# Causal masks moved from TensorE to a VectorE pass, and a token-stationary compression, in a two-layer hybrid transformer

## The chip, the cores and the metric

The kernel runs on one core of one Trainium2 chip. The metric is the device time of one execution in microseconds (us). The core has TensorE (PE in the profile, its weight loads PEld), VectorE (DVE), ScalarE (ACT), GpSimd (POOL) and SyncE (SP, which issues most transfers). Each engine works through its own queue in order and waits on semaphores of the others.

## The reference, cut to what matters

The model has two layers over 512 tokens of width 1024, in float32: an even layer (MoBA and differential attention, 16 score maps), an odd layer (NSA attention, 16 query heads with a selected and a window branch, 32 score maps), and a mixture of experts (MoE) after each. The change touches the causal softmax, which every score map goes through, and the compression of keys and values in the odd layer:

```python
s_own = jnp.where(kpos[None, :] <= qpos[:, None], s_own, NEG_INF)
p = jax.nn.softmax(jnp.concatenate([s_sel, s_own], axis=-1), axis=-1)

def compress_blocks(t, pos_emb, w1, b1, w2, b2):
    idx = jnp.arange(nc)[:, None] * CMP_STRIDE + jnp.arange(CMP_BLOCK)[None, :]   # stride 16, blocks of 32
    blocks = t[:, :, idx, :] + pos_emb.astype(t.dtype)
    hid = jax.nn.gelu(jnp.einsum('bgnld,ldf->bgnf', blocks, w1.reshape(CMP_BLOCK, d, -1)) + b1)
    return jnp.einsum('bgnf,fe->bgne', hid, w2) + b2
```

With 512 tokens all past blocks are selected, so each score map is a causal 512 x 512 one. The adaptive norms take `silu(c) @ ada_w`; the change also touches how `silu(c)` is laid out for it.

## The kernel before

The work runs in stages: modulation and the first projections (0 to 87 us), even attention with its output projection (87 to 345), MoE (to 541), the odd layer's compressions and projections (to about 655), odd attention with its output projection (to 985), MoE (to the end). Weights stream in through a pool of five tiles `w` of 512 KB.

A projection (`product`, line 332) is three matmuls per weight piece, with 256 or 304 columns: weights and activations are split into a high and a low part (`wh`, `wl`, `hTh`, `hTl`) by a cast on ACT (L299) and a subtraction on DVE or POOL (L301).

Scores are computed by `Attn.scores`, per head and per tile i of 128 queries, over n = 128, 256, 384 or 512 keys. Two matmuls (L493) write a PSUM bank `psS` (three banks), a third of 128 columns in bfloat16 (L495) adds the triangular mask `c_k_cmask` to the last 128 columns through the identity `identb`. DVE reduces the bank to the negated maximum `nm` (L497); ACT reads the bank again and writes `exp(s + nm)` into the tile `P` with its row sum in `sm` (L499). Tiles P come from four pools P0 to P3 by width, each with four buffers. DVE inverts the sums (L637, L943, L944), POOL scales P (L507), PE transposes P into `psT` (L520), ACT or DVE copies that to `PT` (L168, L171), and PE multiplies `PT` with the values (L528, L672). These last steps of a head pair stand behind the scores of the next pair. There are 16 + 32 maps with four tiles each: 64 tiles in the even and 128 in the odd layer, 192 in all. While attention runs, the next projection and the modulation units for later (`ada_unit`, L221 and L223, eight DVE passes each) are interleaved as background steps.

The compression (`compress`, L789) runs twice, for keys and values. Per pair of 32 steps of `l` it takes 128 tokens blocks (4 groups x 32, read from `cT` with a stride of 16) against 256 hidden units; the weights are the stationary side, in two halves `fo`, and 64 matmuls in all feed 128 columns each. A float32 matmul shows as two records in the trace. The result `hid` has hidden units on the partitions; bias, gelu and a second matmul follow.

The order on every engine is made at build time by a list scheduler, which goes by priorities and a model of durations. So an edit moves instructions elsewhere too.

Of the kernel before, what the change touches and what calls it, by code (L numbers as in the profile page):

```python
# [9 lines left out]
F32 = mybir.dt.float32  # L10
F32R = mybir.dt.float32r
BF = mybir.dt.bfloat16
I32 = mybir.dt.int32
AF = mybir.ActivationFunctionType
ALU = mybir.AluOpType
AX = mybir.AxisListType

D = 1024
S = 512
NT = 4  # L20
KC = 8
# [3 lines left out]
CAP = 96  # L25
SLOT_TILES = NEXP * CAP // 128
BIG = 8192.0
N_ADA = (3, 7, 7, 7)
N_ADA1 = (2, 2, 4, 3, 5)
PER0 = 6  # L30
# [43 lines left out]
def hybrid_kernel(ctx: ExitStack, tc: tile.TileContext, A: dict, out: bass.AP, dbg=None):  # L74
    nc = tc.nc
# [5 lines left out]
    cst = ctx.enter_context(mkpool("cst"))  # L81
# [4 lines left out]
    def ps(tag, dt=F32):  # L86
        return pp.tile([128, 512], dt, name="ps" + tag, tag=tag, bufs={"S": 3, "P": 2, "T": 2, "O": 1}[tag])
# [26 lines left out]
    ident = identr.bitcast(F32)  # L114
# [10 lines left out]

    late = []

    def load_const(name, shape, dt=F32):

        o = cst.tile(shape, dt, name="c_" + name)  # L130

        def load(pool):
            t = o
            if dt != F32:
                t = pool.tile(shape, F32, name="ctmp", tag=f"P{(shape[1] - 1) // 128}", bufs=4)
            tc.keep_in_program_order(nc.scalar.dma_start(t, A[name]))
            if dt != F32:
                nc.vector.tensor_copy(o, t)
        late.append(load)
        return o  # L140

    ropec = load_const("k_ropec", [128, NT, 16])
    ropes = load_const("k_ropes", [128, NT, 16])
    cmask = load_const("k_cmask", [128, 128], BF)
    zmask = load_const("k_zmask", [128, NT])
    tri = load_const("k_tri", [128, 128], BF)
    iotas = load_const("k_iota", [128, CAP], BF)
# [26 lines left out]
    ct = cst.tile([128, KC], F32, name="ct")  # L174
# [2 lines left out]
    nc.scalar.activation(ce, ct, AF.Exp, scale=-1.0)  # L177
    nc.vector.tensor_scalar(ce, ce, 1.0, None, op0=ALU.add)
    nc.vector.reciprocal(ce, ce)
    cs = cst.tile([128, KC, 32], F32, name="cs")  # L180
    nc.gpsimd.memset(cs, 0.0)
    nc.vector.tensor_tensor(cs[:, :, 0:1], ct[:, :, None], ce[:, :, None], op=ALU.mult)

    modp = [[dr.tile([1, D], F32, name=f"modp{l}_{p}") for p in range(6)] for l in range(2)]
    modg = [[dr.tile([1, D], F32, name=f"modg{l}_{p}") for p in range(2)] for l in range(2)]
# [18 lines left out]
    def ada_half(l, part, c, keep):  # L204

        p = ps("S")
        ts = []
        for q in range(2):
            ts.append(raw_piece(A["ada_w"][l], q, part * D + c * 256, 256))
        for q in QO:  # L210
            for k in range(4):
                nc.tensor.matmul(p[32 * k:32 * k + 32, :256], cs[:, 4 * q + k, :], ts[q][:, k, :],
                                 start=(q == QO[0]), stop=(q == QO[1]), tile_position=(0, 32 * k))
        evac(keep, p[:, :256], 256)

    def ada_unit(l, part, c, pool):


        a = g1[:, c * 256:(c + 1) * 256]
        ts = [raw_piece(A["ada_w"][l], q, part * D + c * 256, 256) for q in range(2)]  # L220
        nc.vector.tensor_scalar(a, ts[0][:, 0, :], cs[:, 0, 0:1], None, op0=ALU.mult)  # L221
        for k in range(1, KC):
            nc.vector.scalar_tensor_tensor(a, ts[k // 4][:, k % 4, :], cs[:, k, 0:1], a, op0=ALU.mult, op1=ALU.add)  # L223
        cost(0, 2600)
        if c == 3:
            p = ps("S")
            for j in range(4):
                nc.tensor.matmul(p[32 * j:32 * j + 32, :256], ones1.to_broadcast([128, 32]),
                                 g1[:, j * 256:(j + 1) * 256], start=True, stop=True, tile_position=(0, 32 * j))
            r = pool.tile([128, 256], F32, name="adap", tag="raw", bufs=2)  # L230
            evac(r, p[:, :256], 256)
            nc.sync.dma_start(modp[l][part].rearrange("a (j c) -> (a j) c", j=4), r[0:128:32, :])
            if part in (2, 5):
                nc.sync.dma_start(modg[l][part // 5].rearrange("a (p k) -> p (a k)", k=KC), mod_col(l, part, f"g{l}_{part}"))
# [175 lines left out]
    class Attn:  # L410
# [69 lines left out]

        def scores(self, qh, kh):

            pool = self.pool
            sm = pool.tile([128, NT], F32, name="sm", tag="sm", bufs=6)
            P = []
            for i in range(NT):
                n = (i + 1) * 128
                tc.cur_priority -= SCP
                if i != 1:
                    bank = ps("S")  # L490
                s = bank[:, 128:384] if i == 1 else bank
                for v in range(2):
                    nc.tensor.matmul(s[:, :n], qh[:, i * 128:(i + 1) * 128], kh[:, v, :n],  # L493
                                     start=(v == 0), stop=False)
                nc.tensor.matmul(s[:, i * 128:n], identb, cmask, start=False, stop=True)  # L495
                nm = pool.tile([128, 1], F32, name="nm", tag="nm", bufs=4)
                nc.vector.tensor_reduce(nm, s[:, :n], axis=AX.X, op=ALU.max, negate=True)  # L497
                e = pool.tile([128, n], F32, name="P", tag=f"P{i}", bufs=4)
                nc.scalar.activation(e, s[:, :n], AF.Exp, bias=nm, accum_out=sm[:, i:i + 1])  # L499
                cost(n / 1.2 + 240, n / 0.96 + 65)  # L500
                P.append(e)
                tc.cur_priority += SCP
            return P, sm
# [31 lines left out]
    def even_attn(l, bp, ns, ada, mlp):  # L535
        with mkpool(f"at{l}") as pool, mkpool(f"top{l}") as top:
# [26 lines left out]
            def affine(c):  # L563

                k2 = slice(2 * c, 2 * c + 2)
                p = ps("O")
                for j in range(2):
                    for k in range(2):
                        nc.tensor.matmul(p[:, 2 * j + k:2 * j + k + 1], parts[1 - j][:, k * 128:(k + 1) * 128], ones1,
                                         start=True, stop=True)  # L570
                nc.vector.tensor_tensor(sb[:, :, k2], p[:, 0:4].rearrange("p (j k) -> p j k", j=2), cols[:, 0:2, k2],
                                        op=ALU.add)
                nc.vector.scalar_tensor_tensor(sb[:, 0, k2], sb[:, 0, k2], 1.0, cols[:, 2, k2], op0=ALU.add, op1=ALU.mult)
# [155 lines left out]
    def odd_attn(l, bp, ns, ada, mlp):  # L729
        s1, b1 = mod_affine(l, 0, 1, A["norm1_g"][l], f"a{l}")  # L730
        with mkpool(f"at{l}") as pool, mkpool(f"top{l}") as top:
# [45 lines left out]

            def compress(a):
                cT = cT2[:, a]
                hid = ps("S")  # L780
                w1 = A["od_cmp_w1"][0, a].rearrange("(h l d) f -> h d l f", h=2, l=16)
                for q in range(4):
                    wt = wp.tile([128, 4, 256], F32, name="w", tag="w", bufs=WB)
                    for hf in range(2):
                        nc.sync.dma_start(wt[64 * hf:64 * hf + 64], w1[hf, :, 4 * q:4 * q + 4, :])
                    for fo in range(2):
                        for li in range(4):
                            lp = 4 * q + li
                            nc.tensor.matmul(hid[:, fo * 128:(fo + 1) * 128], wt[:, li, fo::2],  # L789
                                             cT[:, :, lp::16],  # L790
                                             start=(lp == 0 and fo == 0), stop=(lp == 15),
                                             skip_group_check=True)
                b1c = small([128, 2], "b1c")
                nc.sync.dma_start(b1c, A["od_cmp_b1"][0, a].rearrange("(p o) -> p o", o=2))
                nc.vector.tensor_tensor(b1c, b1c, hid[:, 31:256:128], op=ALU.add)
# [873 lines left out]
```

## Time and profile before

| | |
|---|---|
| median of 3 runs | 1183.71 us (1183.18 to 1186.62) |
| profiled execution | 1184.13 us, span 1182.4 us |
| PE busy | 1089.0 us, 92% of the span |
| DVE busy | 609.0 us, 52% |
| ACT busy | 503.9 us, 43% |
| POOL busy | 279.7 us, 24% |
| mean granted TensorE clock | 0.957 |

The span runs from the first to the last instruction of the profiled execution. Busy time is the union of an engine's instructions. The ends of matmuls are modelled, so their starts say more than their lengths. The queries used below cut the span into windows, name what an engine waited for, and list instructions in order of time.

### The profile page before, as it was taken

What the parts mean: (1) busy time and instruction counts of PE and PEld (TensorE: products, weight loads), DVE (VectorE), ACT (ScalarE), POOL (GpSimd) and SP (SyncE); (2) the same over time, 40 slices, a digit from 0 to 9 for tenths busy, and PEclk for the clock granted to TensorE, in tenths of its full rate; (3) what the DMA queues carried; (4) which work ended last, traced back from release to release, by engine and by line L of the source; (5) the groups of instructions that cost most, each with busy time, mean ns of one, the idle gap of its engine ahead of it and who ended that gap; (6) DMA issues with size and microseconds to landing.
All of it is one profiled execution on the core that took longest, in us unless ns stands there. A gap on an engine that the chain in (4) does not pass through costs nothing. (4 is left out here: it accounts for less than half of the span.)

```text
span 1182.4 us, 21909 instructions
## 1 busy us (share of the span) xinstructions
PE 1089.0 (92%) x8375; PEld 746.2 (63%) x8376; DVE 609.0 (52%) x1602; ACT 503.9 (43%) x1268; POOL 279.7 (24%) x362
## 2 busy tenths in 40 slices
PE   5899999989989899996999998998999998989994
PEld 3798889878764333335999977664577573433332
DVE  2587979884335233226227587536675325322234
ACT  2245656665432222214334565665745442213222
POOL 2200010333231211122001222333434223211223
PEclk8999899999999899996999999998999998989997
DMA  9864657631395899774366354201411094989857
GB/s 272 261 211 154 193 168 217 196 126 55 135 413 163 321 333 410 271 173 95 96 161 195 109 183 122 81 10 37 126 47 62 1 389 185 313 324 385 331 142 180
DMA packets 146086, 226.00 MB, mean 191 GB/s; under 512 B 31822, under 2 KB 116750, under 8 KB 141872
## 3 DMA queue, kind: packets, MB, share of 16 engines
q1 hardware_dynamic: 134400, 195.46, 49.3%
q0 software_dynamic: 10080, 28.46, 8.3%
q8 instruction: 69, 1.13, 0.4%
q10 hardware_dynamic: 1488, 0.55, 0.2%
q14 instruction: 49, 0.40, 0.1%
HBM read 212.73 MB, written 18.93 MB: 196 GB/s over the span
## 5 line engine op out<-in xcount | busy, mean ns | idle before, releaser
L332 PE MATMUL psP<-wh,hTh 128*128 128x256 f32 (+1 forms) x656 | 191.1, 297 | 6.6 <-ACT wh L299 2.8
L332 PE MATMUL psP<-wh,hTl 128*128 128x256 f32 (+1 forms) x656 | 187.2, 289 | 0.4 <-DVE hTl L301 0.4
L332 PE MATMUL psP<-wl,hTh 128*128 128x256 f32 (+1 forms) x656 | 183.0, 290 | 1.3 <-DVE wl L301 1.1
L1256 PE MATMUL psS<-gu,xT 128*32 128x512 f32 x1536 | 176.7, 605 | 0.3
L223 DVE SCALAR_TENSOR_TENSOR g<-w,cs,g 128x256 f32<-128x256 f32 x280 | 140.5, 526 | 2.8 <-DMA w<-in_ada_w_dram 1.7
L507 POOL TENSOR_SCALAR P<-P,sm 128x128 f32<-128x128 f32 (+3 forms) x160 | 97.4, 627 | 153.2 <-DVE sm L944 61.1
L332 PEld LDWEIGHTS psP<-wh,hTh 128*128 128x128 f32 x656 | 127.0, 195 | 8.8 <-ACT wh L299 3.2
L301 POOL TENSOR_TENSOR wl<-w,wh 128x512 fp32r<-128x512 f32 (+1 forms) x38 | 51.2, 1346 | 327.4 <-ACT wh L299 275.1
L332 PEld LDWEIGHTS psP<-wh,hTl 128*128 128x128 f32 x656 | 126.9, 193 | 2.0 <-issue 1.2
L497 DVE TENSOR_REDUCE nm<-psS 128x1 f32<-128x128 f32 x192 | 85.8, 484 | 80.2 <-PE psS L495 75.4
L332 PEld LDWEIGHTS psP<-wl,hTh 128*128 128x128 f32 x656 | 124.3, 194 | 4.3 <-DVE wl L301 3.0
L499 ACT ACTIVATE P<-psS,nm 128x128 f32<-128x128 f32 x192 | 101.6, 534 | 55.0 <-DVE nm L497 53.9
L299 ACT CAST wh<-w 128x512 fp32r<-128x512 f32 (+1 forms) x124 | 75.0, 609 | 111.5 <-PE psP L332 55.5
L1256 PEld LDWEIGHTS psS<-gu,xT 128*32 128x32 f32 x1536 | 55.3, 111 | 100.3 <-issue 92.1
L493 PE MATMUL psS<-kT,qT 128*128 128x512 f32 (+3 forms) x384 | 101.5, 355 | 2.5 <-ACT P L499 2.3
L332 PE MATMUL psP<-wh,o 128*128 128x256 f32 x480 | 95.6, 293 | 0.9 <-ACT o L299 0.7
L301 DVE TENSOR_TENSOR wl<-w,wh 128x512 fp32r<-128x512 f32 (+1 forms) x86 | 58.2, 677 | 63.4 <-ACT wh L299 61.1
L1278 PE MATMUL psP<-dn,sT 128*32 128x512 f32 x768 | 87.8, 595 | 1.0 <-ACT sT L1271 0.8
L168 ACT COPY PT<-psT 128x384 f32<-128x384 f32 (+1 forms) x125 | 62.8, 518 | 47.4 <-PE psT L520 46.7
L332 PEld LDWEIGHTS psP<-wh,o 128*128 128x128 f32 x480 | 75.7, 193 | 9.1 <-issue 5.7
L520 PE MATMUL psT<-identr,P 128*128 128x128 f32 x440 | 72.3, 286 | 3.4 <-ACT PT L168 2.9
L1227 ACT ACTIVATE xT<-psT,bm,sm 128x128 f32<-128x128 f32 x96 | 36.2, 457 | 88.8 <-PE psT L1246 88.8
(334 smaller groups left out, 1801.2 us busy)
## 6 DMA issues: line engine op xcount, KB each, us to landing
w<-in_ada_w_dram SPq DMA_DIRECT2D x96, 512.0 KB
gu<-in_moe_w_gate_dram SPq DMA_DIRECT2D x64, 512.0 KB
gu<-in_moe_w_up_dram SPq DMA_DIRECT2D x64, 512.0 KB
dn<-in_moe_w_down_dram SPq DMA_DIRECT2D x32, 1024.0 KB
w<-in_ev_w_in_dram SPq DMA_DIRECT2D x20, 512.0 KB
w<-in_od_w_in_dram SPq DMA_DIRECT2D x18, 512.0 KB
X<-yD POOLq DMA_DIRECT2D x16, 512.0 KB, 8.3
w<-in_ev_w_out_dram SPq DMA_DIRECT2D x8, 512.0 KB
```

What stands on the lines that cost most here:

```text
L168: nc.scalar.copy(o, i)
L223: nc.vector.scalar_tensor_tensor(a, ts[k // 4][:, k % 4, :], cs[:, k, 0:1], a, op0=ALU.mult, op1=ALU.add)
L299: nc.scalar.copy(hi, src)
L301: o = e.tensor_tensor(lo, src, hi.bitcast(F32), op=ALU.subtract)
L332: nc.tensor.matmul(dst, xx[:, k, tk], ww, start=(k == 0 and v == 0 and i % per == 0), stop=(k == 4 * len(qs) - 1 and v == 2), skip_group_c ...
L493: nc.tensor.matmul(s[:, :n], qh[:, i * 128:(i + 1) * 128], kh[:, v, :n], start=(v == 0), stop=False)
L497: nc.vector.tensor_reduce(nm, s[:, :n], axis=AX.X, op=ALU.max, negate=True)
L499: nc.scalar.activation(e, s[:, :n], AF.Exp, bias=nm, accum_out=sm[:, i:i + 1])
L507: nc.gpsimd.tensor_scalar(P[i], P[i], sm[:, i:i + 1], 1.0, op0=ALU.mult, op1=ALU.mult)
L520: nc.tensor.transpose(t[:, o:o + 128], P[i][:, j * 128:(j + 1) * 128], ident)
L1256: nc.tensor.matmul(hp[c], xT[:, k, c], gu(k), start=(k == 0), stop=(k == KC - 1), tile_position=(0, 32 * q))
L1278: nc.tensor.matmul(yp[g], sT[:, f, g], dn(f, c), start=(f == 0), stop=(f == 1), tile_position=(0, 32 * q))
```

## The change

1. The mask matmul goes. DVE runs one pass per tile instead of the reduce: it reads the scores from PSUM and the mask from SBUF, writes `-(s + mask)` into P and keeps the minimum, which is the negated maximum. This pass shows as two instructions, the pass and the read-out of its one value per partition. The exponential then works in place on P, with scale -1. `cmask` becomes 512 columns wide, 384 zeros and the triangle, so that its last n columns fit any tile.
2. In the compression the tokens become the stationary side and the weights are fed, 256 contiguous columns at a time: 32 matmuls. The result has tokens on the partitions; it is copied to SBUF (`hb`) and transposed back by four transpositions into `psT`.
3. `cs` (the activated `c`) loses its zero padding to 32 columns and is broadcast instead, so all 32 rows of a modulation product are equal, and the sum over them uses 1/32 (`part1`) instead of ones.

```diff
+    cmask = cst.tile([128, 512], BF, name="cmask")
+    nc.gpsimd.memset(cmask[:, 0:384], 0.0)
+    load_const("k_cmask", [128, 128], BF, cmask[:, 384:512])
...
-    cs = cst.tile([128, KC, 32], F32, name="cs")
-    nc.gpsimd.memset(cs, 0.0)
-    nc.vector.tensor_tensor(cs[:, :, 0:1], ct[:, :, None], ce[:, :, None], op=ALU.mult)
+    cs = cst.tile([128, KC], F32, name="cs")
+    nc.vector.tensor_tensor(cs, ct, ce, op=ALU.mult)
+    part1 = cst.tile([128, 1], F32, name="part1")
+    nc.gpsimd.memset(part1, 1.0 / 32)
...
                 for v in range(2):
                     nc.tensor.matmul(s[:, :n], qh[:, i * 128:(i + 1) * 128], kh[:, v, :n],
-                                     start=(v == 0), stop=False)
-                nc.tensor.matmul(s[:, i * 128:n], identb, cmask, start=False, stop=True)
+                                     start=(v == 0), stop=(v == 1))
                 nm = pool.tile([128, 1], F32, name="nm", tag="nm", bufs=4)
-                nc.vector.tensor_reduce(nm, s[:, :n], axis=AX.X, op=ALU.max, negate=True)
                 e = pool.tile([128, n], F32, name="P", tag=f"P{i}", bufs=4)
-                nc.scalar.activation(e, s[:, :n], AF.Exp, bias=nm, accum_out=sm[:, i:i + 1])
+                nc.vector.tensor_tensor_reduce(e, s[:, :n], cmask[:, 512 - n:], -1.0, -MASKED, ALU.add, ALU.min, nm)
+                nc.scalar.activation(e, e, AF.Exp, bias=nm, scale=-1.0, accum_out=sm[:, i:i + 1])
...
-                    for fo in range(2):
-                        for li in range(4):
-                            lp = 4 * q + li
-                            nc.tensor.matmul(hid[:, fo * 128:(fo + 1) * 128], wt[:, li, fo::2],
-                                             cT[:, :, lp::16],
-                                             start=(lp == 0 and fo == 0), stop=(lp == 15),
-                                             skip_group_check=True)
+                    for li in range(4):
+                        lp = 4 * q + li
+                        nc.tensor.matmul(hw[:, :256], cT[:, :, lp::16], wt[:, li, :], start=(lp == 0), stop=(lp == 15))
+
+                hb = top.tile([128, 256], F32, name="hb", tag="raw", bufs=2)
+                evac(hb, hw[:, :256], 256)
+                hid = ps("T")
+                for fo in range(2):
+                    nc.tensor.transpose(hid[:, fo * 128:(fo + 1) * 128], hb[:, fo::2], ident)
```

Nine lines more in the file move later line numbers: L332 becomes L339, L493 L501, L497 L505, L499 L506, L507 L514, L520 L527, L528 L535, L789 L795, the transpositions of `hb` are L801.

The first place is PE at the first compression of the odd layer; L771 (L778) are transpositions of the value tokens, `w` the weights. Before:

```order
L775 MATMUL psO<-identr,posr 128x16
L789 MATMUL psS<-cT_7026,w 128x128
L771 MATMUL psT<-identr,craw 64x128 x4
L789 MATMUL psS<-cT_7026,w 128x128 x11
L771 MATMUL psT<-identr,craw 64x128 x4
L789 MATMUL psS<-cT_7026,w 128x128 x12
L771 MATMUL psT<-identr,craw 64x128 x8
L789 MATMUL psS<-cT_7026,w 128x128 x8
L332 MATMUL psP<-wh,hTh 128x304
```

And now:

```order
L782 MATMUL psO<-identr,posr 128x16
L795 MATMUL psS<-w,cT_6964 128x256
L778 MATMUL psT<-identr,craw 64x128 x4
L795 MATMUL psS<-w,cT_6964 128x256 x10
L778 MATMUL psT<-identr,craw 64x128 x4
L795 MATMUL psS<-w,cT_6964 128x256 x5
L339 MATMUL psP<-wh,hTh 128x304
L339 MATMUL psP<-wh,hTl 128x304
```

32 matmuls of 128 columns become 16 of 256, and the second half of the transpositions has left this place.

The second place is PE late in the odd attention, at the scores of one head of the third group; P_9740 to P_9756 before, and P_9591 to P_9611 now, are the tiles of the head that held the same four buffers. Before:

```order
L493 MATMUL psS_10116<-kT_7649,qT_9112 128x384 x2
L495 LDWEIGHTS identb_83
L495 MATMUL psS_10116<-c_k_cmask_89,identb_83 128x128
L520 MATMUL psT_10036<-identr_76,P_9740 128x128
L520 MATMUL psT_10036<-identr_76,P_9748 128x128
L520 MATMUL psT_10036<-identr_76,P_9756 128x128
L520 MATMUL psT_10041<-identr_76,P_9748 128x128
L520 MATMUL psT_10041<-identr_76,P_9756 128x128 x2
L528 MATMUL psO_9802<-PT_10027,vw_7024 64x512
L493 MATMUL psS_10124<-kT_7649,qT_9112 128x512 x2
L495 LDWEIGHTS identb_83
L495 MATMUL psS_10124<-c_k_cmask_89,identb_83 128x128
```

And now:

```order
L501 MATMUL psS_9965<-kT_7565,qT_8996 128x512 x2
L892 MATMUL psT_9728<-identr_76,pc_9721 128x128 x4
L527 MATMUL psT_9874<-identr_76,P_9591 128x128
L527 MATMUL psT_9874<-identr_76,P_9597 128x128
L527 MATMUL psT_9874<-identr_76,P_9604 128x128
L527 MATMUL psT_9874<-identr_76,P_9611 128x128
L527 MATMUL psT_9880<-identr_76,P_9597 128x128
L527 MATMUL psT_9880<-identr_76,P_9604 128x128
L527 MATMUL psT_9880<-identr_76,P_9611 128x128
L501 MATMUL psS_9945<-kT_7565,qT_8996 128x256 x2
L527 MATMUL psT_9885<-identr_76,P_9604 128x128
L527 MATMUL psT_9885<-identr_76,P_9611 128x128 x2
```

The masks are gone, and the 512-key scores, which stood behind the transpositions of the tile P_9756 whose buffer they follow, now stand ahead of those of P_9604 and P_9611.

The third place is DVE for the tiles of that same head; `g1` is a modulation unit, and the brackets name the engines whose semaphores an instruction waits for. Before:

```order
L221 TENSOR_SCALAR g1_70<-w_10427,cs_107 128x256 [waits DMAHW2_49]
L497 TENSOR_REDUCE nm_10112<-psS_10101 128x1 [waits PE_49]
L497 TENSOR_REDUCE nm_10120<-psS_10116 128x1
L497 TENSOR_REDUCE nm_10128<-psS_10124 128x1
L223 SCALAR_TENSOR_TENSOR g1_70<-w_10287,cs_107,g1_70 128x256 [waits DVE_49]
L242 TENSOR_TENSOR sn1_10647<-sn1_10647,mcb_10649 128x8 [waits DMAHW3_49]
```

And now:

```order
L505 ISA P_9949,nm_9948<-psS_9945,cmask_89 128x128 [waits PE_49,Pool_49]
L505 ISA nm_9948 128x1
L230 SCALAR_TENSOR_TENSOR g1_70<-w_10257,cs_108,g1_70 128x256 [waits DVE_49]
L249 TENSOR_TENSOR bn1_10473<-bn1_10473,mcb_10475 128x8 [waits DMAHW7_49,DMAHW3_49]
L230 SCALAR_TENSOR_TENSOR g1_70<-w_10257,cs_108,g1_70 128x256 [waits DVE_49]
L505 ISA P_9955,nm_9954<-psS_9945,cmask_89 128x256 [waits PE_49,Pool_49]
L505 ISA nm_9954 128x1
L505 ISA P_9962,nm_9961<-psS_9958,cmask_89 128x384 [waits PE_49,Pool_49]
L505 ISA nm_9961 128x1
L505 ISA P_9969,nm_9968<-psS_9965,cmask_89 128x512 [waits PE_49,Pool_49]
L505 ISA nm_9968 128x1
L952 RECIPROCAL sm_9944<-sm_9944 128x4 [waits Activation_49]
```

Each reduce has become a pass with its read-out, and the pass waits for PE and POOL, where three reduces in a row had one wait for PE.

## Rows read from the trace of the kernel before

**Rows 1.** stages; window, its length, busy time of each engine, granted clock, DMA

```profile
core 0: us, PE busy (x) PEld busy (x) DVE busy (x) ACT busy (x) POOL busy (x), PEclk, DMA share, GB/s
...
87.00:215.00 128.00, 123.99 (x1000) 113.20 (x999) 106.14 (x286) 77.31 (x211) 14.47 (x13) 0.97 0.62 188
...
579.00:655.00 76.00, 75.43 (x520) 74.05 (x519) 34.56 (x86) 26.41 (x59) 7.70 (x8) 1.00 0.57 158
...
690.00:780.00 90.00, 84.17 (x589) 61.39 (x582) 59.12 (x151) 50.16 (x131) 24.95 (x36) 0.96 0.38 116
780.00:947.00 167.00, 158.60 (x1036) 106.43 (x1035) 94.35 (x228) 97.89 (x274) 61.36 (x94) 0.97 0.16 50
```

**Rows 2.** the waits of PE in 655 to 947: total, times, longest

```profile
PE psP L332 <- DVE wl L301: 3.8, 3, 2.7
...
PE psS L493 <- ACT P L499: 2.3, 5, 0.8
```

**Rows 3.** timeline of PE, odd attention: start, length, what, how many

```profile
665.16 0.63 PE L493 MATMUL psS<-kT,qT 128*128 128x512 f32 x2
665.63 0.23 PE L495 MATMUL psS<-c_k_cmask,identb 128*128 128x128 bf16 x1
665.66 0.36 PE L332 MATMUL psP<-wl,hTh 128*128 128x256 f32 x1
665.87 0.28 PE L332 MATMUL psP<-wh,hTh 128*128 128x256 f32 x1
665.99 0.28 PE L332 MATMUL psP<-wh,hTl 128*128 128x256 f32 x1
```

**Rows 4.** timeline of PE, two later places of the odd attention

```profile
911.03 0.23 PE L495 MATMUL psS<-c_k_cmask,identb 128*128 128x128 bf16 x1
911.07 0.71 PE L493 MATMUL psS<-kT,qT 128*128 128x512 f32 x2
911.62 0.23 PE L495 MATMUL psS<-c_k_cmask,identb 128*128 128x128 bf16 x1
...
921.89 0.23 PE L495 MATMUL psS<-c_k_cmask,identb 128*128 128x128 bf16 x1
921.96 0.82 PE L520 MATMUL psT<-identr,P 128*128 128x128 f32 x6
```

**Rows 5.** the compression's line among groups by shape: busy, mean ns, idle before

```profile
L789 PE MATMUL psS<-cT,w 128*128 128x128 f32 x128 | 29.4, 394 | 0.0
```

**Rows 6.** timeline of PE during the first compression

```profile
586.08 5.41 PE L789 MATMUL psS<-cT,w 128*128 128x128 f32 x24
591.32 1.05 PE L771 MATMUL psT<-identr,craw 128*64 128x128 f32 x8
```

**Rows 7.** timeline of PE in the first MoE

```profile
361.12 3.25 PE L1324 MATMUL psS<-X,oh 128*128 128x512 f32 x7
```

**Rows 8.** the page's costliest groups: the maximum pass and the exponential

```profile
L497 DVE TENSOR_REDUCE nm<-psS 128x1 f32<-128x128 f32 x192 | 85.8, 484 | 80.2 <-PE psS L495 75.4
...
L499 ACT ACTIVATE P<-psS,nm 128x128 f32<-128x128 f32 x192 | 101.6, 534 | 55.0 <-DVE nm L497 53.9
```

**Rows 9.** groups by shape: passes of VectorE, small ones, and ScalarE's

```profile
L499 ACT ACTIVATION_READ_ACCUMULATOR P<-psS,nm 128x1 f32 x192 | 38.9, 203 | 0.0
...
L497 DVE TENSOR_REDUCE nm<-psS 128x1 f32<-128x512 f32 x48 | 32.7, 681 | 3.6 <-PE psS L495 3.6
...
L168 ACT COPY PT<-psT 128x512 f32<-128x512 f32 x41 | 24.1, 587 | 30.3 <-PE psT L520 30.2
...
L986 DVE TENSOR_TENSOR X<-psP,X 128x512 f32<-128x512 f32 x28 | 19.0, 689 | 24.4 <-PE psP L332 24.4
...
L1537 ACT ACTIVATE xs<-X 128x512 f32<-128x512 f32 x16 | 9.9, 622 | 15.0 <-DVE X L1536 14.9
...
L1313 DVE TENSOR_REDUCE rsl<-psO 128x1 f32<-128x3 f32 x22 | 3.3, 151 | 0.0
...
L662 DVE SCALAR_TENSOR_TENSOR P<-P,sm 128x512 f32<-128x512 f32 x4 | 3.0, 746 | 0.0
```

More of the change, by code (lines that the diff above doesn't have):

```diff
@@ L27 @@
 BIG = 8192.0
+MASKED = -1e30
 N_ADA = (3, 7, 7, 7)
@@ L126, in hybrid_kernel, with load_const @@
     late = []
-    def load_const(name, shape, dt=F32):
-        o = cst.tile(shape, dt, name="c_" + name)
+    def load_const(name, shape, dt=F32, o=None):
+        if o is None:
+            o = cst.tile(shape, dt, name="c_" + name)
         def load(pool):
@@ L143, in hybrid_kernel @@
     ropes = load_const("k_ropes", [128, NT, 16])
-    cmask = load_const("k_cmask", [128, 128], BF)
+    cmask = cst.tile([128, 512], BF, name="cmask")
+    nc.gpsimd.memset(cmask[:, 0:384], 0.0)
+    load_const("k_cmask", [128, 128], BF, cmask[:, 384:512])
     zmask = load_const("k_zmask", [128, NT])
@@ L211, in ada_half @@
             for k in range(4):
-                nc.tensor.matmul(p[32 * k:32 * k + 32, :256], cs[:, 4 * q + k, :], ts[q][:, k, :],
+                nc.tensor.matmul(p[32 * k:32 * k + 32, :256], cs[:, 4 * q + k:4 * q + k + 1].to_broadcast([128, 32]), ts[q][:, k, :],
                                  start=(q == QO[0]), stop=(q == QO[1]), tile_position=(0, 32 * k))
@@ L220, in ada_unit @@
         ts = [raw_piece(A["ada_w"][l], q, part * D + c * 256, 256) for q in range(2)]
-        nc.vector.tensor_scalar(a, ts[0][:, 0, :], cs[:, 0, 0:1], None, op0=ALU.mult)
+        nc.vector.tensor_scalar(a, ts[0][:, 0, :], cs[:, 0:1], None, op0=ALU.mult)
         for k in range(1, KC):
-            nc.vector.scalar_tensor_tensor(a, ts[k // 4][:, k % 4, :], cs[:, k, 0:1], a, op0=ALU.mult, op1=ALU.add)
+            nc.vector.scalar_tensor_tensor(a, ts[k // 4][:, k % 4, :], cs[:, k:k + 1], a, op0=ALU.mult, op1=ALU.add)
         cost(0, 2600)
@@ L568, in affine @@
                     for k in range(2):
-                        nc.tensor.matmul(p[:, 2 * j + k:2 * j + k + 1], parts[1 - j][:, k * 128:(k + 1) * 128], ones1,
+                        nc.tensor.matmul(p[:, 2 * j + k:2 * j + k + 1], parts[1 - j][:, k * 128:(k + 1) * 128], part1,
                                          start=True, stop=True)
@@ L779, in compress @@
                 cT = cT2[:, a]
-                hid = ps("S")
+                hw = ps("S")
                 w1 = A["od_cmp_w1"][0, a].rearrange("(h l d) f -> h d l f", h=2, l=16)
```

## The prediction

> **What bounds the kernel now.** I read the stages first, then the waits of PE, then single matmuls in the timeline, and the groups by shape last. In the stages [rows 1] compare PE's busy time with the length of each window. In both attention stages and around the compressions it is almost all of it: 123.99 of 128, 75.43 of 76, 84.17 of 90 and 158.60 of 167 us. DVE is near that only in the first (106.14 of 128), and DMA never (0.16 to 0.62). The waits agree: from 655 to 947 us PE's longest total is 3.8 us, for a split on DVE, and 2.3 us for a bank that the exponential holds [rows 2]. So PE's own work is the bound there, and what leaves PE shortens the time unless another engine then ends last. A busy share hides how dense PE is, so the prices come from starts, not from busy times.
>
> **The masks leave PE.** 192 mask matmuls go, with a weight load each. In rows 3 the mask starts at 665.63, 0.47 us after the two score matmuls. The projection matmul behind it starts 0.03 us later, but the next one only at 665.87: it holds PE for 0.21 us where its follower holds it for 0.12 (665.87 to 665.99). The mask costs 0.03 + 0.09 = 0.12 us. Before another pair of scores it is the same: from 911.07 to 911.62 a pair of 512 columns takes 0.55 us instead of 0.47, and the mask ahead took 0.04 [rows 3, 4]. Before a transposition it is the 0.07 us between 921.89 and 921.96 [rows 4]. By the order of before, 72 masks stand ahead of a projection, 50 ahead of a score, 42 ahead of a transposition, 28 ahead of others, which I price at the bare 0.04: 122 x 0.12 + 42 x 0.07 + 28 x 0.04 = 18.7 us. Bounds: 192 x 0.03 = 5.8, if the slower start of the matmul behind stays without the mask, and 192 x 0.12 = 23.0.
>
> [...]
>
> **The compressions.** 64 fp32 calls of 128 columns are 128 records [rows 5]; 24 of them run from 586.08 to 591.32, 0.218 us each [rows 6], so 27.9 us. They feed the tokens with a stride of 16. Afterwards 32 calls, 64 records, feed 256 contiguous columns of weights, and the tokens are the stationary side. The nearest row for fp32 columns fed contiguously is L1324: 7 records of 512 columns in 3.25 us [rows 7], 0.46 each, so 0.23 for 256: 64 x 0.23 = 14.9. Four transpositions, 8 records, at most 0.218 each, add 1.7. Saved: 27.9 - 14.9 - 1.7 = 11.3 us. From below: if a column costs what it does in rows 6 whatever its stride, 64 x 0.436 = 27.9 and 1.7 is lost. I take the gain, since L1324 has the same type and the contiguous feed. The copy hb and the transpositions are a longer chain, but in the order the transpositions stand 35 and 23 rows behind the last matmul of their compression, with projection between, and PE is busy there (75.43 of 76).
>
> **What VectorE takes over.** Each of the 192 reduces becomes two instructions. The reduce takes 484 ns in the mean [rows 8]. Nearest to the new pass, which reads PSUM and SBUF and writes SBUF, is L986: 689 ns at 512 columns where the reduce takes 681; with a scalar and two SBUF sources L662 takes 746 [rows 9]. The read-out of one value I take like a reduce over three, 151 ns; from above like ScalarE's read-out, 203 [rows 9]. So 0.16 us more per tile (0.008 + 0.151), at most 0.27 (0.065 + 0.203): 30 to 52 us of DVE in all. Even if 40 of the even layer's 64 tiles fall into 87 to 215, that is 6.4 to 10.7 us against 21.9 idle there [rows 1]; in the other windows the cover is wider. I cost the length at nothing; without the cover it would be these 30 to 52 us.
>
> The exponential now reads SBUF: 622 ns at 512 columns (L1537) against 587 from PSUM (L168) [rows 9], some 0.035 x 192 = 6.7 us of ScalarE, hidden by its 97.89 busy of 167. The PSUM bank is free after the pass rather than after the exponential, 534 ns earlier [rows 8]; this can return up to the 2.3 us of rows 2 and is not counted. The zeros in cmask, the broadcast cs and part1 touch the start and the modulation alone: a memset goes and two come on POOL, matmuls keep their number. Nothing.
>
> **What is given back.** The pass writes the probability tile, which the exponential did before. So VectorE's queue, not ScalarE's, now waits until the transpositions of the tile four before in that buffer are done. By the order, in 55 of the 128 tiles of the odd layer these stand behind the tile's own scores on PE; before it was so in 15. The two places shown with the change are one such head: P_9969 waits for PE and POOL; behind it on DVE stand its read-out, the reciprocal of the head's sums, and later splits of projection weights, for which ScalarE's exponential, POOL's scaling and PE's projections wait. No row shows such a wait. From below it is nothing (or the 2.3 us gained above). From above, 32 heads of four passes at 0.64 us, 2.5 us per head, all exposed, would be 81 us. The nearest rows are what PE idles now beside such chains: 5.8 us in 690 to 780 and 8.4 in 780 to 947 [rows 1], 14.2 us over the odd layer's 128 tiles, most of them scored there, 0.11 per tile. I let each of the 55 cost that once more: 6.1 us.
>
> **Sum.** -18.7 - 11.3 + 6.1 = -23.9 us, against the profiled execution's 1184.13 us (its span 1182.4 and 1.7 around it), which is 0.4 above the median 1183.71. Forecast 1160 us.
>
> **Rivals.**
> - Nothing is given back: DVE's idle time swallows the waits. 1184.1 - 30.0 = 1154. For it: PE has projection matmuls between the scores in most places. Against: PE idles already where these are few.
> - The compression gains nothing, as priced from below: 1160 + 11.3 + 1.7 = 1173. For it: no row feeds 256 fp32 columns against strided weights. Against: rows 7.
> - The new pass takes two steps per element. The part of the reduce above the 151 ns doubles: +0.33, with the read-out +0.48 per tile. In 87 to 215 forty tiles make 106.1 + 19.4 = 125.5 us of DVE, as much as the shortened window (128 less 40 x 0.1) holds. That window loses its 4 us, and about half of DVE's 21.9 idle, which waits make, is added: 1160 + 4 + 11 = 1175. Against: L662 has two SBUF sources and is 746, not double [rows 9]. [...]
> - Slower: the passes stuck at the probability buffers starve PE. Place: the odd attention, 32 heads. Each head's passes come after the transpositions instead of during them; PE then meets transpositions whose tiles are not ready. It decides from 30.0 / 32 = 0.94 us of PE wait per head. At 1.5 us the time is 1184.1 - 30.0 + 48 = 1202. For it: 55 late tiles, four-deep buffers. Against: a pair of heads lies between scores and use, and PE's waits for these chains are small now [rows 2].
>
> **Chances.** Forecast with some give-back (1155 to 1167) 0.45; nothing given back 0.22; compression without gain 0.09; two steps per element 0.11; starved 0.13. A difference under 0.3% can't be told from none here. Faster by more: the first three and most of the fourth, 0.84. Within: 0.04, the fourth with dearer waits. Slower: 0.12. The range, 1150 to 1181, takes in all but the last and the far ends of the bounds.
>
> **What would show it.** Right: no mask rows, and projection matmuls behind scores at 0.12 us from the first on; L795 as 64 records near 0.23 us; passes near L986 by shape with read-outs of 0.15 us; DVE under 0.95 busy in the even attention; PE's waits for P or PT in the odd attention at about twice now's. Wrong: L795 near 0.44 us; passes above 1 us at 512 columns; PE idle in the odd attention up by 30 us or more, ended by VectorE or by a transposition's evacuation.

## The result and the profile after

The changed kernel takes 1168.84 us (median of 4 runs, 1167.9 to 1173.3) where the kernel before took 1183.45 beside it. The ratio is 0.9884, with a 95% interval from 0.9847 to 0.9921: 14.6 us faster, between 9 and 18. The forecast was 1160, within 1150 to 1181. The profiled execution took 1168.73 us, with a span of 1167.0.

The stages first, with the columns of [rows 1]. The windows start where those of before do, and the last two end earlier, as the stages do.

```profile
core 0: us, PE busy (x) PEld busy (x) DVE busy (x) ACT busy (x) POOL busy (x), PEclk, DMA share, GB/s
87.00:215.00 128.00, 117.65 (x934) 109.42 (x934) 105.24 (x318) 76.59 (x205) 14.18 (x10) 0.96 0.59 179
579.00:643.00 64.00, 62.41 (x444) 60.83 (x445) 32.89 (x83) 26.56 (x60) 6.68 (x8) 1.00 0.66 188
690.00:780.00 90.00, 83.08 (x536) 61.43 (x537) 54.35 (x178) 55.94 (x149) 26.23 (x41) 0.94 0.29 90
780.00:936.00 156.00, 140.88 (x900) 96.51 (x899) 89.72 (x286) 89.78 (x246) 53.31 (x85) 0.96 0.20 62
```

PE was busy for 123.99 of the first 128 us before and is for 117.65 now; in the last stage it idles 15.1 us where it idled 8.4. So PE was given time and did not fill it.

I summed PE's time from the start of one matmul to the next, and counted what an interval has above 0.65 us as a wait. The compressions and the projections around them, from the odd layer's first transposition to its first score, fell from 114.6 to 104.5 us. The two attentions, each from its first score to the first matmul of its MoE, fell only from 592.8 to 589.9: their matmuls by 16.3 us, and their waits grew by 13.4 (22.1 to 35.5). Of the 15.4 us between the two spans, then, 10.1 lie in the compressions' place, 2.9 in the attentions and 2.4 in the other stages. This is one trace of each kernel, and the executions of the kernel before alone spread from 1178 to 1191 us, so a few us in one stage can be chance.

The compression's group by shape, which answers to [rows 5], and two rows of PE's timeline, which answer to [rows 6]:

```profile
L795 PE MATMUL psS<-w,cT 128*128 128x256 f32 x64 | 16.2, 398 | 0.3 <-DVE cT L783 0.3
```

```profile
583.65 1.95 PE L795 MATMUL psS<-w,cT 128*128 128x256 f32 x8
585.43 0.60 PE L778 MATMUL psT<-identr,craw 128*64 128x128 f32 x4
585.87 2.48 PE L795 MATMUL psS<-w,cT 128*128 128x256 f32 x10
588.00 0.49 PE L339 MATMUL psP<-wh,hTh 128*128 128x304 f32 x1
```

Eight records from 583.65 to 585.43 are 0.22 us each, ten from 585.87 to 588.00 are 0.21. A record feeds 256 columns now and took 0.218 before with 128.

VectorE's pass and ScalarE's exponential by shape, with [rows 8, 9]:

```profile
L506 ACT ACTIVATE P<-P,nm 128x512 f32<-128x512 f32 x48 | 34.3, 715 | 1.4 <-DVE nm L505 1.4
...
L505 DVE CUSTOM_DVE_ANT_0 P<-psS,cmask 128x512 f32<-128x512 f32 x48 | 33.0, 687 | 3.5 <-PE psS L501 3.5
...
L505 DVE DVE_READ_ACCUMULATOR2_ANT nm<- 128x1 f32 x192 | 16.2, 84 | 0.1
```

The pass takes 687 ns where the reduce took 681, and its read-out 84. The exponential takes 715 where it took 695 (before's group of that shape).

PE's timeline in the odd attention, without a mask between scores and projection (compare [rows 3]):

```profile
653.71 0.33 PE L501 MATMUL psS<-kT,qT 128*128 128x384 f32 x1
653.88 0.28 PE L339 MATMUL psP<-wh,hTl 128*128 128x256 f32 x1
654.00 0.28 PE L339 MATMUL psP<-wl,hTh 128*128 128x256 f32 x1
654.12 0.28 PE L339 MATMUL psP<-wh,hTh 128*128 128x256 f32 x1
```

The projection starts every 0.12 us from the first on, so the slower start behind a mask (0.21 us in [rows 3]) is gone. What PE waits for instead stands in its waits, from 640 to 986 (compare [rows 2]):

```profile
PE psT L892 <- POOL pc L888: 9.8, 2, 9.3
PE psT L480 <- ACT kT L173: 4.0, 1, 4.0
PE psS L501 <- DVE nm L505: 3.4, 4, 2.0
PE psP L339 <- ACT raw L452: 3.1, 2, 3.0
```

One wait has 9.3 of the 13.4 us. PE, GpSimd and VectorE there, from the timeline (VectorE's without the rows between):

```profile
804.73 0.74 PE L501 MATMUL psS<-kT,qT 128*128 128x512 f32 x2 [1.95 <-DVE nm L505]
814.75 1.11 PE L892 MATMUL psT<-identr,pc 128*128 128x128 f32 x4 [9.29 <-POOL pc L888]
```

```profile
809.85 3.67 POOL L514 TENSOR_SCALAR P<-P,sm 128x128 f32<-128x128 f32 x4 [7.45 <-DVE sm L953]
813.50 1.21 POOL L888 TENSOR_TENSOR pc<-pc,cm 128x512 f32<-128x512 f32 x1
```

```profile
803.39 0.68 DVE L882 TENSOR_TENSOR pc<-psT,cm 128x512 f32<-128x512 f32 x1
...
804.59 1.27 DVE L230 SCALAR_TENSOR_TENSOR g<-w,cs,g 128x256 f32<-128x256 f32 x3
...
806.25 0.68 DVE L884 TENSOR_REDUCE cm<-pc 128x16 f32<-128x512 f32 x1
806.85 0.47 DVE L230 SCALAR_TENSOR_TENSOR g<-w,cs,g 128x256 f32<-128x256 f32 x1
...
808.63 0.25 DVE L885 RECIPROCAL cm<-cm 128x16 f32<-128x16 f32 x1
808.80 0.79 DVE L230 SCALAR_TENSOR_TENSOR g<-w,cs,g 128x256 f32<-128x256 f32 x2
809.50 0.16 DVE L953 TENSOR_TENSOR sm<-sm,gt 128x4 f32<-128x4 f32 x1
809.58 0.87 DVE L230 SCALAR_TENSOR_TENSOR g<-w,cs,g 128x256 f32<-128x256 f32 x2
810.37 0.28 DVE L887 TENSOR_TENSOR cm<-cm,gt 128x16 f32<-128x16 f32 x1
```

The small steps that make pc (L882, L884, L885, L887) and sm (L953) stand on VectorE between products of modulation units (L228, L230), 0.40 us apart. Between L882 and L887 there are 11 of these; the order of before has 6. GpSimd scales four P tiles, released by sm, and only then pc: L887 ends at 810.65, but the tiles keep GpSimd until 813.50, so some 2.9 us of the wait are GpSimd's order. PE's next instruction is the transposition of pc, and everything behind it waits too. So my theory for the experiments: VectorE's modulation units, which hid beside PE, no longer do once the masks have left PE. The rivals: the two parts of the change clash; the new pass costs it; the masks' time was never on the path.

### The profile page after: what moved, and what is told of

Its sections match the earlier page's. It is cut to its first block, busy times and chain, and to the rows that moved or that the text cites. A ratio compares the mean times of both kernels' runs of the same rounds, so it can differ in the third digit from the quotient of the medians.

```text
span 1167.0 us, 21574 instructions
## 1 busy us (share of the span) xinstructions
PE 1061.1 (91%) x8123; PEld 732.7 (63%) x8124; DVE 608.9 (52%) x1795; ACT 509.6 (44%) x1269; POOL 274.9 (24%) x363
## 5 line engine op out<-in xcount | busy, mean ns | idle before, releaser
L339 PE MATMUL psP<-wh,hTh 128*128 128x256 f32 (+1 forms) x656 | 189.4, 294 | 7.9 <-ACT raw L452 4.1
L339 PE MATMUL psP<-wh,hTl 128*128 128x256 f32 (+1 forms) x656 | 187.7, 289 | 0.9 <-DVE hTl L308 0.9
L339 PE MATMUL psP<-wl,hTh 128*128 128x256 f32 (+1 forms) x656 | 182.4, 290 | 1.8 <-DVE wl L308 1.6
L230 DVE SCALAR_TENSOR_TENSOR g<-w,cs,g 128x256 f32<-128x256 f32 x280 | 142.0, 532 | 3.6 <-DMA w<-in_ada_w_dram 2.5
L339 PEld LDWEIGHTS psP<-wh,hTh 128*128 128x128 f32 x656 | 127.1, 195 | 11.4 <-ACT raw L452 5.4
L339 PEld LDWEIGHTS psP<-wh,hTl 128*128 128x128 f32 x656 | 127.3, 194 | 3.9 <-issue 2.4
L505 DVE CUSTOM_DVE_ANT_0 P<-psS,cmask 128x128 f32<-128x128 f32 x192 | 87.5, 488 | 81.2 <-PE psS L501 52.1
L514 POOL TENSOR_SCALAR P<-P,sm 128x128 f32<-128x128 f32 (+3 forms) x160 | 92.6, 597 | 154.0 <-DVE sm L953 81.3
L339 PEld LDWEIGHTS psP<-wl,hTh 128*128 128x128 f32 x656 | 124.5, 194 | 4.9 <-DVE wl L308 2.8
L506 ACT ACTIVATE P<-P,nm 128x128 f32<-128x128 f32 x192 | 107.1, 559 | 39.1 <-DVE nm L505 38.5
L501 PE MATMUL psS<-kT,qT 128*128 128x512 f32 (+3 forms) x384 | 96.5, 350 | 5.5 <-DVE nm L505 5.4
L339 PE MATMUL psP<-wh,o 128*128 128x256 f32 x480 | 94.1, 290 | 1.7 <-ACT wh L306 0.8
L339 PEld LDWEIGHTS psP<-wh,o 128*128 128x128 f32 x480 | 75.4, 191 | 12.3 <-issue 7.1
L527 PE MATMUL psT<-identr,P 128*128 128x128 f32 x440 | 73.6, 289 | 3.7 <-ACT PT L173 2.9
L501 PEld LDWEIGHTS psS<-kT,qT 128*128 128x128 f32 x384 | 62.4, 195 | 20.2 <-DVE nm L505 10.1
```

The costliest lines, as they stand in the source:

```text
L339: nc.tensor.matmul(dst, xx[:, k, tk], ww, start=(k == 0 and v == 0 and i % per == 0), stop=(k == 4 * len(qs) - 1 and v == 2), skip_group_c ...
L505: nc.vector.tensor_tensor_reduce(e, s[:, :n], cmask[:, 512 - n:], -1.0, -MASKED, ALU.add, ALU.min, nm)
L506: nc.scalar.activation(e, e, AF.Exp, bias=nm, scale=-1.0, accum_out=sm[:, i:i + 1])
L514: nc.gpsimd.tensor_scalar(P[i], P[i], sm[:, i:i + 1], 1.0, op0=ALU.mult, op1=ALU.mult)
L527: nc.tensor.transpose(t[:, o:o + 128], P[i][:, j * 128:(j + 1) * 128], ident)
```

## The experiments

Each median is set against that of the kernel before, measured beside it: 1182.84 us for the runs named e, 1184.04 for those named h and r_after, 1183.12 for p_even, p_all and u_odd, 1183.71 for u_before. The intervals are of the ratio to it. Lengths of stages and waits come from one trace of each kernel.

**e1_compress and e2_pass: each part alone.** The first is the kernel before with the new body of compress, the second the changed kernel with the old one (so it has the third part of the change, `cs`, too):

```
-                nc.tensor.matmul(hid[:, fo * 128:(fo + 1) * 128], wt[:, li, fo::2], cT[:, :, lp::16], ...
+                nc.tensor.matmul(hw[:, :256], cT[:, :, lp::16], wt[:, li, :], ...
```

> The kernel before with the new compressions alone. My theory (the compressions' saving is whole, since VectorE and ScalarE are idle beside them): 11 to 13 us faster than before, 1170 to 1172. In the trace the 64 compression matmuls run about 0.22 us apart, and nothing else changes place. Rival (the new compressions are given back too, and what the changed kernel gained came from the scores): 1181 to 1185.

> The changed kernel with the old compressions: VectorE's pass in place of the mask matmuls, and nothing else. My theory (PE gets its 18.7 us of mask matmuls back, and loses 16 of them in waits, 9 at one place): 1179 to 1183, 1 to 4 us faster than before, with one wait of about 9 us for pc near 810 us. Rival (the two parts only clash when put together; alone the pass keeps its gain): 1164 to 1170.

Measured: 1175.67, ratio 0.9937 (0.9916 to 0.9958), and 1176.40, ratio 0.9940 (0.9914 to 0.9966). Both miss. Alone the compressions are worth 7.2 us and the pass 6.4; together 13.6, within the error of the 14.6, so the parts do not clash. In the trace of e1 the compressions' stretch is 10.8 us shorter (114.6 to 103.8), as forecast, and the attentions are 3.3 longer, so a part of this gain too seems to be given back. In the trace of e2 the attentions are 4.1 us shorter, with the wait for pc that was expected (9.3 us, ending at 825.9); the rest of its gain lies in stages that it does not touch.

**e3_nomask: the masks leave PE, VectorE does nothing for it.**

```
-                                     start=(v == 0), stop=False)
-                nc.tensor.matmul(s[:, i * 128:n], identb, cmask, start=False, stop=True)
+                                     start=(v == 0), stop=(v == 1))
```

> The kernel before without the mask matmuls and without anything in their place: the causal mask is left out, and the maximum is found by the old reduction. It prices the mask matmuls on PE alone. If the path is PE's and nothing but VectorE's pass gives time back: 1163 to 1167 (18.7 us less, and what the clock adds). If PE's gain is lost whatever VectorE does, because the loads of weights or the other engines set the pace: 1176 to 1183. Half and half, about 1172, would say that a part of what was given back has nothing to do with the pass.

Measured: 1181.58, ratio 0.9993 (0.9978 to 1.0008). 192 matmuls less on PE are worth nothing that can be told, as the second of the three expectations had it (its reason, that VectorE does not matter, fails in h_nomask below). That clears the pass: with it (e2) and without it (e3) the attentions take 588.7 and 588.4 us. In all, e2 is even 5.2 us faster than e3; in the traces that lies in the two MoE stages, which neither touches. ScalarE's splits of projection weights from 87 to 215 us, before and then in e3, show who waits:

```profile
L299 ACT CAST wh<-w 128x512 fp32r<-128x512 f32 x26 | 16.0, 622 | 12.4 <-DMA w<-in_ev_w_in_dram 4.2 <-PE psP L332 2.7 <-DVE P L662 2.1
```

```profile
L299 ACT CAST wh<-w 128x512 fp32r<-128x512 f32 x26 | 16.0, 622 | 22.9 <-DMA w<-in_ev_w_in_dram 17.8 <-PE psP L332 4.7 <-ACT P L498 0.3
```

They wait 17.8 us for weights to land, where it was 4.2. SyncE's queue of loads in the same window, before and then in e3 (L345 issues projection weights, L201 those of the units):

```profile
SPq L201 <- DVE g L223: 31.0, 16, 4.5
...
SPq L345 <- DVE g L223: 8.2, 5, 3.4
```

```profile
SPq L201 <- DVE g L223: 26.5, 11, 6.4
SPq L345 <- DVE g L223: 19.8, 9, 8.8
```

Projection and units share a ring of five weight buffers. A projection's load that needs a buffer of a unit waits until VectorE has used it up: 19.8 us now against 8.2. So in the even attention of e3 VectorE's units reach PE by way of the weights. In the changed kernel the two figures are 7.6 us (ScalarE for weights to land) and 8.9 (these loads for the units), near those of before, so its trace does not show this path.

**h_before, h_nomask, h_after: half of the units' products left out**, in the kernel before, in e3 and in the changed kernel:

```
-        for k in range(1, KC):
+        for k in range(2, KC, 2):
```

> The kernel before with half of the modulation units' products left out (4 of 8 input slices in each unit; the loads stay), which takes some 65 us of work from VectorE, most of it in the two attentions. It is the base for the next two. Theory (VectorE's queue, and the weight buffers that it holds in it, is what PE meets next): 1165 to 1178. Rival (PE alone bounds the attentions): 1181 to 1185.

> The same with the mask matmuls left out too (the causal mask is missing, the old reduction finds the maximum). With all of the units' work, leaving the masks out was worth 1 us. Theory (VectorE's units ate PE's gain): 10 to 18 us under h_before. Rival (the masks' time on PE was never on the path, or the waits are for ScalarE and the order of instructions): 0 to 4 us under h_before.

> The changed kernel with half of the units' products left out. Theory (VectorE's units ate it): 23 to 30 us under h_before, twice what the change gave with all of the units' work (14). Rival (the give-back has another cause): 12 to 16 us under h_before, as with all of the units' work.

Measured: 1184.58, ratio 0.9990 (0.9973 to 1.0006); 1173.29, 0.9903 (0.9884 to 0.9922); 1155.51, 0.9760 (0.9738 to 0.9782). The first lies where the rival put it, the other two where the theory did. Some 80 us less work on VectorE (L230 falls from 142.0 us in the changed kernel to 60.9) do not change the time of the kernel before, against my expectation: there the amount of VectorE's work is no bound. The same cut makes the changed kernel 13.3 us faster. With room on VectorE the masks are worth 11.3 us (1.3 without it), and the whole change 29.1 (14.6 without it). So it is shown that the units' work takes back a part of what the change gives. The order of instructions differs in each of these kernels and can have a share in the sizes.

Where it does so is less clear for the masks alone. With all of the products the attentions take 592.8 us before, 588.4 in e3 and 589.9 in the changed kernel; with half of them 596.9, 586.3 and 573.7. So with room the whole change gains 23.2 us there and not 2.9. But from e3 to h_nomask the attentions gain only 2.1 of the 8.1 us between the spans, and a part of the 11.3 is that h_before's attentions are 4.1 us longer than before's. The kernels that leave something out compute other values, by which the MoE then sends the tokens; its two stages take 382.6 to 388.7 us together in these kernels and 383.7 to 389.5 in the others, so that is hardly the cause.

PE's matmuls from 87 to 215 us, for e3, h_nomask and h_after:

```profile
87.00:215.00 128.00, 117.03 (x935) 108.14 (x934) 104.21 (x282) 73.09 (x202) 11.79 (x10) 0.97 0.60 179
```

```profile
87.00:215.00 128.00, 120.31 (x971) 113.03 (x970) 83.89 (x224) 77.01 (x215) 14.97 (x14) 0.97 0.64 190
```

```profile
87.00:215.00 128.00, 124.42 (x1026) 117.28 (x1025) 88.73 (x285) 84.43 (x236) 19.12 (x19) 0.99 0.67 202
```

Before, 40 of the 1000 were masks, so 960 others, and in h_before 958. With the masks gone PE does no more of them in that time while VectorE has all of its products (935 in e3, 934 in the changed kernel), and more with half (971 in h_nomask, 1026 in h_after). This is the clearest sign that the units hold PE in this window. Over the whole even attention h_after is 7.4 us shorter than the changed kernel, but h_nomask no shorter than e3 (269.7 and 268.9). VectorE's waits at the P buffers do not explain it: they are 22.1 us in the changed kernel, and more in h_after, which is 13 us faster:

```profile
DVE P L505 <- PE psT L527: 22.1, 16, 3.2
```

```profile
DVE P L505 <- PE psT L527: 28.3, 20, 3.8
```

h_nomask and h_after differ by the compressions, the pass and `cs`: 17.8 us, more than the compressions' 11. PE's waits from 640 to 986 of h_nomask have scores that wait for a bank until the exponential has read it:

```profile
PE psS L493 <- ACT P L498: 3.9, 7, 1.4
```

In h_after these are 3.1 us and end with the pass. That the earlier release is the rest of the 17.8 is argued only; the three traces cannot part it from the order of instructions. The wait for pc is still 6.7 us in h_after, so the amount of the units' work alone does not make it.

**r_after: one buffer more for the units.**

```
+        own = pool is even_top[0]
...
+                        t=pool.tile([128, 4, 256], F32, name="wu", tag="wu", bufs=1) if q and own else None) for q in range(2)]
```

> The changed kernel with one buffer more for weights in the even attention: the second tile of a modulation unit gets a buffer of its own and leaves the shared ring of five. Theory (in the even attention the loads of projection weights wait in SyncE's queue behind those of the units, whose buffers VectorE frees late, and this holds PE where the masks left): SyncE waits less for VectorE, and the even attention gets 3 to 8 us shorter: 1161 to 1166. Rival (weights come early enough; the time is lost elsewhere): 1167 to 1171.

Measured: 1194.96, ratio 1.0098 (1.0081 to 1.0116): 26 us slower than the changed kernel, which neither side expected. The waits of SyncE's queue and of PE from 80 to 352 us:

```profile
SPq L208 <- DVE g L234: 46.8, 19, 5.6
...
SPq L208 <- DMA wu<-in_ada_w_dram: 19.1, 6, 4.5
```

```profile
PE psS L239 <- DVE g L234: 10.3, 4, 7.8
```

A single own buffer lets only one unit's second tile be under way; units end later, and PE, in order, waits 10.3 us for their sums (L239), where it waited 0.3 in the changed kernel. It shows that the units' pace reaches PE, but not what a longer ring would give, which was not tried. How much goes by the ring and how much by VectorE's own queue stays open.

**e4_units, u_odd and u_before: the units dealt out otherwise** (the last in the kernel before):

```
-N_ADA1 = (2, 2, 4, 3, 5)
+N_ADA1 = (2, 2, 4, 4, 4)     # e4_units
+N_ADA1 = (3, 2, 4, 3, 4)     # u_odd, u_before
```

> The changed kernel with one modulation unit moved from the third group of the odd attention to the last but one list (2, 2, 4, 4, 4 in place of 2, 2, 4, 3, 5). By the order of instructions VectorE then has none of the units' operations between the two steps that make pc in the third group, where the changed kernel has 11 and the kernel before 6. My theory (the wait of 9.3 us for pc is VectorE's queue, filled with units ahead of pc's last steps): the wait falls under 3 us, and the time by 6 to 9 us, to 1160 to 1163. Rival (the wait is made by GpSimd, which scales four P tiles before pc, or moves to another place): 1166 to 1170.

> The changed kernel with the odd attention's units dealt out as 3, 2, 4, 3, 4. By the order of instructions VectorE has none of their operations between pc's steps in three of four groups and 7 in the first. Where e4_units had a new wait of 4.4 us for the pass at 834 us, this has the same five units less one in the fourth list. Theory (any long run of units on VectorE puts off something that PE waits for, wherever it stands): the wait for pc falls under 3 us, others grow, and the time is 1165 to 1170. Rival (only the place beside pc mattered): 1158 to 1163.

> The kernel before with the odd attention's units dealt out as 3, 2, 4, 3, 4, as u_odd has them. Theory (with the mask matmuls on PE, VectorE had time for the units wherever they stood; the deal matters only since PE is faster): 1180 to 1185, no change. Rival (the new deal is better for any kernel, and u_odd's gain of 7.6 us has nothing to do with the change): 1173 to 1177.

e4_units: 1168.97, ratio 0.9886 (0.9860 to 0.9912), no gain over the changed kernel. Its waits of PE from 640 to 986:

```profile
PE psS L501 <- DVE nm L505: 6.0, 4, 4.4
PE psT L892 <- POOL pc L888: 3.3, 2, 2.5
```

The wait for pc fell from 9.3 to 2.5 us, as my theory has it, and another of 4.4 came in: the gain moved, as the rival had it. The pass that PE waits for there starts at 838.66 on VectorE, and what it stands behind are not units but nine products of the output projection's weights with the gate, background work of the same queue:

```profile
831.71 7.03 DVE L358 TENSOR_TENSOR w<-w,g 128x512 f32<-128x512 f32 x9 [1.19 <-DMA g<-modg]
```

u_odd: 1161.28, ratio 0.9795 (0.9765 to 0.9826). It beats the kernel before by 21.8 us and the changed one by 7.6, more than I expected. That is in the rival's range, but not by its reason, as the waits for pc still sum to 6.7 us where the changed kernel has 9.8. One unit is done ahead of the odd attention, and no wait there is above 3.6:

```profile
PE psT L892 <- POOL pc L888: 6.7, 3, 3.4
PE psT L460 <- DVE qst L308: 3.6, 1, 3.6
```

u_before: 1178.66, ratio 0.9957 (0.9938 to 0.9975), 5.1 us faster than before, between both expectations. So most of u_odd's 7.6 has nothing to do with the change: the deal also takes waits from the odd attention of before (13.8 to 9.1 us). With it the change is worth 17.4 us, which the intervals do not tell from 14.6.

**p_even and p_all: products moved to GpSimd**, in the even attention, or in both:

```
+        for k in range(nk, KC):
+            t = ts[1][:, k - 4, :]
+            nc.gpsimd.tensor_scalar(t, t, cs[:, k:k + 1], 1.0, op0=ALU.mult, op1=ALU.mult)
+            nc.gpsimd.tensor_tensor(a, a, t, op=ALU.add)
```

> The changed kernel with the last 3 of the 8 products of each modulation unit of the even attention done by GpSimd (a product and an addition each) in place of VectorE. Nothing is left out. VectorE loses 24 units by 3 by 0.40 us = 29 us there, GpSimd gets 24 by 3 by about 1.3 us = 93 us and is idle for most of that stage. Theory (VectorE's queue holds PE in the even attention since the masks left): 3 to 7 us under the changed kernel, 1162 to 1166. Rival (a unit takes longer, since GpSimd's chain ends it, and its buffers come free later): 1168 to 1175.

> The same for the units of both attentions. Theory: 6 to 11 us under the changed kernel, 1158 to 1163, and the wait of 9.3 us for pc in the odd attention is at most half as long, since only 5 of the units' operations stand between pc's steps on VectorE and not 11. Rival (in the odd attention GpSimd scales the P tiles, and the units' products delay them, so PE's transposes wait): 1166 to 1175.

Measured: 1187.27, ratio 1.0027 (1.0002 to 1.0052), and 1197.10, ratio 1.0108 (1.0074 to 1.0142), worse than the rivals. The groups of GpSimd and VectorE in p_all:

```profile
L236 POOL TENSOR_TENSOR g<-g,w 128x256 f32<-128x256 f32 x120 | 97.1, 816 | 37.7 <-DVE g L231 30.1 <-DVE sm L670 4.1
...
L235 POOL TENSOR_SCALAR w<-w,cs 128x256 f32<-128x256 f32 x120 | 76.4, 652 | 88.9 <-DMA w<-in_ada_w_dram 61.4 <-DVE wl L313 8.6 <-DVE g L231 6.3
```

```profile
L231 DVE SCALAR_TENSOR_TENSOR g<-w,cs,g 128x256 f32<-128x256 f32 x160 | 91.2, 583 | 2.4 <-DMA w<-in_ada_w_dram 1.2
```

A product and its addition take 1.47 us on GpSimd (652 and 816 ns), where about 1.3 had been estimated, so a unit's tile is held longer by 3 x (1.47 - 0.40) = 3.2 us, and GpSimd itself waits 61.4 us for weights. The wait for pc in p_all is 9.7 us, though five of the units' products stand between pc's steps on VectorE and not eleven, so that expectation missed too. VectorE's busy time alone is not what counts, then; that the buffers, held longer, are the cause is argued from these numbers, not shown.

## Why the prediction was right, and where not

- **The bound.** Right in that less work on VectorE changes nothing in the kernel before (h_before). But PE's work is not all of it: another deal of the units takes 5.1 us from the same kernel (u_before). What the prediction left out is how near the next bound is.
- **The masks, 18.7 us.** Right in the main as PE's time: without them the matmuls of the two attentions take 16.3 us less (12.7 in e3), and what follows runs at 0.12 us from the first on. In the kernel's time only 1.3 us come of it (e3), or 11.3 with room on VectorE (h_nomask). From the start of a mask to the next start it is 18.7 us in all before (5.3 in the even layer and 13.4 in the odd), but that this is the forecast number is luck: five of these intervals, 0.40 to 1.95 us long, are mostly waits and make 6.0 us of it, and the slower start of the matmul behind a mask is not in it. The measured 16.3 and 12.7 us both lie under the forecast 18.7.
- **The compressions, 11.3 us.** The size is right in its place (10.1 in the changed kernel, 10.8 in e1), with records of 256 columns 0.21 to 0.22 us apart. That the contiguous feed makes it was the prediction's estimate and is not shown. Alone they bring 7.2.
- **VectorE's part, costed at nothing.** The length was overestimated: 0.09 us per tile (687 + 84 against 681 ns), not 0.16, and the pass is no burden (e2 against e3). The failed step is beside it: VectorE's cover was judged by busy shares of stages, for the new pass alone. The work that PE's masks had covered, the modulation units, was not asked after.
- **Given back, 6.1 us.** The mis-sized term: 15.4 us, the -30.0 of the first two terms against the 14.6 measured. In the trace the two terms are 26.4 us of PE's time (16.3 and 10.1) and not 30.0, and the waits in the attentions grew by 13.4. Its place was wrong as well. The P buffers do hold the passes (22.1 us of VectorE's idle time), but PE hardly: its waits for PT in the odd attention came to about twice those of before, as forecast, and to no more than some 1 us. It is given back where PE meets pc, weights, or a pass behind VectorE's background work; how much at each is open.
- **Rivals.** With half of the products left out the sum without give-back comes true, 29.1 us against 30.0, in part by luck: in the traces 23.2 us of it are the attentions', costed at 18.7, and 8.6 the compressions', costed at 11.3. Two steps per element: no (687 ns at 512 columns). Starved passes: no.
- **The range.** 1168.8 lies outside 1155 to 1167, the case of the forecast itself. What the range holds above that was there for the rivals without gain from the compression and with two steps per element, and neither came true.

## What to carry to other kernels

When the bound engine loses work, ask which engine's work was hidden beside it, and check that in the queue's order at each place where the bound engine waits, not in busy shares: an engine at 52% can hold another at 91%. A cheap experiment helps beforehand: leave out the work of the bound engine, with and without half of the suspected engine's. Background work in an in-order queue is worth dealing out with an eye to the small steps behind it on which the bound engine waits; but measure each deal, since here one gave 7.6 us and another only moved the wait.

## What the runs showed of the hardware

- During the wait of 9.3 us the granted clock fell to 0.50, and it stayed there for the first matmuls behind the wait. A window of the changed kernel, with the columns of [rows 1], and two rows of PE's timeline behind the wait:

```profile
807.00:820.00 13.00, 5.25 (x18) 3.43 (x18) 11.97 (x39) 4.80 (x14) 4.85 (x5) 0.50 0.71 184
```

```profile
815.66 1.79 PE L527 MATMUL psT<-identr,P 128*128 128x128 f32 x7
...
820.35 0.66 PE L527 MATMUL psT<-identr,P 128*128 128x128 f32 x4
```

  PE works again from 814.75 on, still at 0.50 until 820.0. The seven transpositions from 815.66 to 817.10 start 0.21 us apart, the four from 820.35 to 820.76 0.10, where the granted clock is 0.97 (820 to 825). So this wait cost more than its 9.29 us.
- The read-out of VectorE's accumulator takes 84 ns; that of ScalarE's exponential takes 190 (203 before).
- An fp32 matmul record that feeds 256 contiguous columns takes 0.21 to 0.22 us, as long as one of 128 columns with a stride of 16. The weight side changed with it (weights with a stride of 2 before, tokens with a stride of 16 now), so the runs do not part the two.
- VectorE's products take longer in the mean where GpSimd does some beside it: 583 ns in p_all, 560 in p_even, 532 in the changed kernel.
